# A two-layer hybrid flow-matching step: side tasks in smaller steps, a later deadline for modulations, and array tilings in the planner's estimate

## The chip, the cores and the metric

One core of one Trainium2 chip. The time is that of one execution in device microseconds (us); the median of several runs stands for a kernel. Engines are named as in the profile: PE (TensorE) multiplies, PEld is its weight load, DVE (VectorE), ACT (ScalarE) and POOL (GpSimd) do elementwise work, SP (SyncE) issues most of the DMAs.

## What is computed

Two layers run over 128 context tokens and 256 latent tokens, width 1024. A layer has a token mixer and a squared-ReLU MLP, each with an RMSNorm before and after it and with shift, scale and gain vectors ("modulations") that come from a condition vector:

```python
m = jax.nn.silu(cond) @ ada_w + ada_b        # six parts of 1024
h = rmsnorm(x, norm_mix_pre) * (1.0 + sc1) + sh1
y = mixer(h)                                 # z = h @ w_in, 12 branch inputs of 512, 4 gates of 1024
x = x + g1 * rmsnorm(y, norm_mix_post)
h = rmsnorm(x, norm_ffn_pre) * (1.0 + sc2) + sh2
x = x + g2 * rmsnorm(square(relu(h @ mlp_w1)) @ mlp_w2, norm_ffn_post)
```

The mixer has four branches: A, a neighbourhood attention; B, a differential attention; C, a retention in both directions, whose decay matrices are exponentials of distances; D, a short convolution over time followed by a gated linear recurrence (RG-LRU) in both directions. Each branch's result is multiplied by its own matrix `w_branch`, weighted with a sigmoid gate, and the sum goes through `w_out`.

## The kernel before, in words

All 384 tokens stay on the chip, mostly as channels by tokens. Float32 matrices are split into two parts of a faster type, a high part (wh) and the rest (wl), and each product is made of three matmuls (high by high, low by high, high by low). A weight load of 1 MB ("raw", two buffers) is split piece by piece: one copy for wh on ACT or DVE, one subtraction for wl on DVE or POOL (`split`, line 504).

The program is one list of pieces of weights, `run_stream` (line 626): for each piece the splits ahead of it are issued (`prepare`, `ahead`), its `pre` function, if it has one, is called, and then its matmuls are issued. A projection piece has 8 x 3 matmuls into one of two "mm" PSUM banks and then an eviction; a branch piece has two times 4 x 3 matmuls of 384 columns, each followed by an eviction (`acc` for branch B, `th` for the others). `triple` (line 865) yields after every 6 matmuls.

The mixer's order of pieces is: values of B, queries and keys of B, the convolution's input (`lx_evac`, line 1141), the LRU's gate (`lg_evac`), the retention's gate and values, gate and branch pieces of B ("yB"), queries and keys of C, gate and branch pieces of D ("yD"), values, queries and keys of A, gate and branch pieces of C ("yC") and of A ("yA"), and the output projection `add_out` (line 1573), whose last four pieces run with the norms that follow in `out_tail` (line 1592).

Everything else runs as side tasks: Python generators put into a list by `later` (line 587) with a tag and a capacity. After each yield of the matmuls `poll` (line 606) goes over the active tasks and advances each by one step, when what it needs is ready by the planner's own clock and when DVE and ACT are at most 2.25 us behind PE there; the tasks tagged "ada" come last and have a limit of their own. So a step's instructions stand in each engine's queue where the poll put them, and an eviction that follows in the program waits behind them. `drain_side(tag)` (line 619) advances tasks until none with the tag is left; `need_y` (line 1523) does so before the first branch piece of each branch. LRU tiles have capacity 7 and retention pairs 6 of the 8 that may be active together.

The planner's clock (`Clock`, and `Engine.cost` from line 167) gives each instruction a price. A matmul of plain float32 costs the larger of its columns / 585 and 0.22 us, and where it uses a part of the array that its caller names, this times its share of 128 output rows.

Side tasks that matter here:

- `lx_evac`: copies the bank to `xp` and runs the convolution, a TENSOR_SCALAR and three SCALAR_TENSOR_TENSOR on DVE, in the eviction itself.
- `lru_tile` (line 1188): per direction two times two matmuls on halves of the array, activations on ACT, products on DVE; then, in one step, for each direction a multiply and two scans on DVE, and two adds and two products.
- `ret_pair` (line 1290): the first step builds two decay matrices (four DVE operations, two exponentials on ACT) and the scaled queries.
- `ada` (line 779): the modulation vectors. For each of 8 x 2 blocks of a 1024-column part a load of 256 KB and two DVE accumulations, then `ada_end` with matmuls, transposes and small DMAs. The plan (line 1792) starts the parts 2, 3 and 4 of a layer within its mixer.
- `need_y` of the last branch also drains "ada", loads the three tiles of x (0.5 MB each) and the four gain tiles (0.25 MB each) through SP, and computes the scale columns.

Of the kernel before, what the change touches and what calls it, by code (L numbers as in the profile page):

```python
# [10 lines left out]
F32R = mybir.dt.float32r  # L11
# [122 lines left out]
def _size(a):  # L134
    n = 1
    for s in a.shape[1:]:
        n *= s
    return n


class Engine:


    def __init__(self, clock, raw, key):
        self.clock, self.raw, self.key = clock, raw, key

    def __getattr__(self, name):
# [19 lines left out]
    def cost(self, name, aps, k):  # L167
# [10 lines left out]
        if self.key == "PE":  # L178
            n = _size(aps[0])
            if name == "transpose":  # L180
                return 0.107
            if aps[1].dtype == F32R:
                return max(n / 2195, 0.107)
            return max(n / 585, 0.22) * (aps[0].shape[0] / 128 if "tile_position" in k else 1)
        if name == "reciprocal":
# [13 lines left out]
def hybrid_flow_kernel(ctx: ExitStack, tc: tile.TileContext, I, O):  # L199
# [734 lines left out]
    def add_layer(l):  # L934
# [206 lines left out]
        def lx_evac(j, p):  # L1141
            xp = atile()
            pool.memset(xp[:, 0:1], 0.0)
            pool.memset(xp[:, 129:131], 0.0)
            pool.memset(xp[:, 387:389], 0.0)
            dve.tensor_copy(xp[:, 1:129], p[:, 0:128])
            dve.tensor_copy(xp[:, 131:387], p[:, 128:384])
            xd = ctile("setB_x")
            cw = lambda i: P("pp")[:, R_CW + 4 * i + j:R_CW + 4 * i + j + 1]
            dve.tensor_scalar(xd[:, 0:NL], xp[:, 0:NL], cw(0), P("pp")[:, R_CB + j:R_CB + j + 1], op0=ALU.mult, op1=ALU.add)  # L1150
            for i in range(1, 4):
                dve.scalar_tensor_tensor(xd[:, 0:NL], xp[:, i:NL + i], cw(i), xd[:, 0:NL], op0=ALU.mult, op1=ALU.add)
            S["xd"][j] = xd

# [32 lines left out]

        def lru_tile(j):
            xd = S["xd"][j][:, 0:NL]
            while "kl" not in LP[l]:  # L1190
                yield
            yield (xd, *S["bia"])
# [33 lines left out]
            for d in range(2):  # L1226
# [4 lines left out]
                for s, init in ((slice(0, 128), 0.0), (slice(130, 386), st)):  # L1231
# [3 lines left out]
                    dve.tensor_tensor_scan(oo, aa, uu, init, ALU.mult, ALU.add)  # L1235
                hs.append(h)
            pool.tensor_copy(hst[:, j:j + 1], hs[0][:, 127:128])
            pool.tensor_copy(hst[:, 4 + j:5 + j], hs[1][:, 0:1])
            gg = S["gg"][j]
            for s, o in ((slice(0, 128), slice(0, 128)), (slice(130, 386), slice(128, 384))):  # L1240
                dve.tensor_add(hs[0][:, s], hs[0][:, s], hs[1][:, s])
                dve.scalar_tensor_tensor(gg[:, o], hs[0][:, s], 0.5, gg[:, o], op0=ALU.mult, op1=ALU.mult)
            S["yD"][j] = gg[:, 0:NTOK]
            if j == 3:
# [45 lines left out]
        def ret_pair(j):  # L1290
# [3 lines left out]
            for hh in range(2):  # L1294
# [5 lines left out]
                act(a, a, AF.Exp)  # L1300
                Dm.append(a)
            qx = []
            io = cst[:, C_IO:C_IO + 256]
# [202 lines left out]
        def add_gate_branch(bi, ykey, first, last):  # L1506
# [16 lines left out]
            def need_y():  # L1523
                drain_side(ykey)
                if last:
                    drain_side("ada")
                    S["X"] = [load_x_tile(l, t) for t in range(3)]
                    S["G"] = gain_tiles(l, 1)
                    S["A2"], S["B2"] = scale_cols(MOD[l, 4], pps[l], R_FFN), MOD[l, 3]

# [33 lines left out]
        def out_mm(k, t, hi, lo, banks=(0, 1)):  # L1564
            mh, ml = S["M"]
            tk = slice(t * 128, (t + 1) * 128)
            for n in banks:
# [3 lines left out]
                mm(p, mh[:, k, tk], wl, start=False, stop=k == KT - 1)  # L1571

        def add_out():
            def piece(k):
# [8 lines left out]
            for k in range(0, KT, 2):  # L1583
                src = I["w_out"][l][k * 128:(k + 2) * 128].rearrange("(k p) c -> p k c", p=128)
                add_load(src, lambda raw: raw.rearrange("p (k c) -> p k c", k=2),
                         [((lambda v, s=s: v[:, s]), (lambda t: t), piece(k + s), None)
                          for s in range(2)])
# [330 lines left out]
```

## Time and profile before

| | us |
|---|---|
| median of 3 runs | 1726.16 |
| lowest and highest run | 1722.91, 1727.71 |
| profiled execution, its own time | 1721.72 |
| its span in the profile | 1719.9 |
| PE busy in the span | 1661.3 |
| DVE busy | 1170.9 |
| ACT busy | 697.2 |

The profile is one execution. A line of it gives the time from the span's start, the duration, the engine, the operation, the tiles written and read, the shapes and a count; in square brackets stands how long the engine was idle before, and what ended that. The granted clock (PEclk) is TensorE's, as a share of full speed. All instructions come from one helper line (L151), so tiles tell them apart: `mm` and `y` are PSUM banks, `acc` and `th` evicted sums, `setB_x` the convolution's result, `tmp` working tiles, `half` and `big` the buffers of modulations, and x.

### The profile page before, as it was taken

The page shows a single profiled execution, that of the slowest core. Times are in us where ns is not written, and L with a number is a line of the kernel's source. Part 1 is how long each engine was busy: PE and PEld are TensorE (multiplying, and loading weights), DVE is VectorE, ACT ScalarE, POOL GpSimd, SP SyncE. Part 2 cuts the span into 40 slices and gives each one's busy share as a digit, 9 for nine tenths or more (in the row PEclk, how much of TensorE's full clock was granted, in tenths as well). Part 3 has the DMA queues.
Part 4 walks back from the last instruction along what each step waited for, and adds up shares of the span by engine and source line. Part 5 has one row for each costly group of instructions (what it writes and reads, how often), then busy time and mean ns, then how long its engine had stood idle before and what let it go on. Part 6 is the DMA issues. An engine that isn't in the chain of part 4 may idle for free.

```text
span 1719.9 us, 24255 instructions
## 1 busy us (share of the span) xinstructions
PE 1661.3 (97%) x9370; PEld 1492.2 (87%) x9370; DVE 1170.9 (68%) x2030; ACT 697.2 (41%) x1352; POOL 227.7 (13%) x298
## 2 busy tenths in 40 slices
PE   6999989999999999999999999999999999999998
PEld 4989879889789899898899887898888998898997
DVE  4586578998565746877677866787786666475444
ACT  4335555233332543333362446532343337333333
POOL 3211000322220100000021200013412101000000
PEclk8999999999999999999999999999999999999999
DMA  9432234458425425665453322453673442454332
GB/s 348 137 105 80 98 100 164 163 169 206 100 99 184 147 93 171 213 208 183 162 165 105 104 99 74 147 179 133 174 210 84 138 169 99 134 202 154 123 123 86
DMA packets 181124, 250.84 MB, mean 146 GB/s; under 512 B 21777, under 2 KB 126018, under 8 KB 181010
## 3 DMA queue, kind: packets, MB, share of 16 engines
q1 hardware_dynamic: 167234, 240.66, 41.1%
q0 software_dynamic: 3936, 5.94, 2.8%
q10 hardware_dynamic: 9840, 2.71, 0.7%
q8 instruction: 73, 1.20, 0.3%
q14 instruction: 41, 0.34, 0.1%
HBM read 243.47 MB, written 5.81 MB: 145 GB/s over the span
## 4 chain that ended last, share of the span: by engine, by line
PE 81%; DVE 8%; DMA 4%; ACT 3%; issue 3%; POOL 1%; SPq 0%; DVEq 0%; ACTq 0%; POOLq 0%
PE mm L151 48%; PE y L151 33%; DVE wl L151 2%; DMA half<-in_ada_w 2%; DVE tmp L151 2%; DVE big L151 1%; ACT tmp L151 1%; DMA half<-in_ada_b 1%; DMA wh<-in_ada_w 1%; ACT wh L151 1%; DVE half L151 1%; DVE setB_x L151 0%; ACT half L151 0%; DVE acc L151 0%; DVE small L151 0%
## 5 line engine op out<-in xcount | busy, mean ns | idle before, releaser
L151 PE MATMUL mm<-hh,wh 128*128 128x384 f32 x1536 | 537.2, 350 | 23.0 <-DVE acc L151 18.0
L151 PE MATMUL mm<-hh,wl 128*128 128x384 f32 x1536 | 520.7, 339 | 1.3 <-DVE wl L151 1.3
L151 PE MATMUL mm<-hl,wh 128*128 128x384 f32 x1536 | 520.4, 339 | 0.0
L151 DVE TENSOR_TENSOR wl<-raw,wh 128x1024 fp32r<-128x1024 f32 x313 | 394.4, 1262 | 163.2 <-ACT wh L151 155.5
L151 ACT ACTIVATE wh<-raw 128x1024 fp32r<-128x1024 f32 x249 | 262.2, 1055 | 224.9 <-PE y L151 139.7
L151 PEld LDWEIGHTS mm<-hh,wh 128*128 128x128 f32 x1536 | 290.7, 189 | 50.2 <-issue 21.1
L151 PEld LDWEIGHTS mm<-hl,wh 128*128 128x128 f32 x1536 | 290.6, 189 | 1.6
L151 PEld LDWEIGHTS mm<-hh,wl 128*128 128x128 f32 x1536 | 290.1, 189 | 1.6 <-DVE wl L151 1.6
L151 DVE SCALAR_TENSOR_TENSOR big<-half,condT,big 128x512 f32<-128x512 f32 x224 | 160.8, 755 | 15.0 <-DMA half<-in_ada_w 14.9
L151 PE MATMUL y<-wh,yh 128*128 128x512 f32 x312 | 123.4, 396 | 0.0
L151 PE MATMUL y<-wh,yl 128*128 128x512 f32 x312 | 123.4, 396 | 0.0
L151 PE MATMUL y<-wl,yh 128*128 128x512 f32 x312 | 123.3, 395 | 0.0
L151 PE MATMUL mm<-yh,wh 128*128 128x384 f32 x256 | 89.5, 350 | 3.2 <-DVE th L151 3.0
L151 POOL TENSOR_TENSOR small<-small,mhalf 128x1 f32<-128x1 f32 (+2 forms) x40 | 35.2, 883 | 413.2 <-DVE small L151 413.2
L151 DVE CAST wh<-raw 128x1024 fp32r<-128x1024 f32 x67 | 46.4, 692 | 61.0 <-PE mm L151 57.3
L151 PE MATMUL mm<-yh,wl 128*128 128x384 f32 x256 | 86.3, 337 | 0.0
L151 PE MATMUL mm<-yl,wh 128*128 128x384 f32 x256 | 86.2, 337 | 0.0
L151 ACT ACTIVATE tmp<-mm 128x384 f32<-128x384 f32 x64 | 31.4, 491 | 135.1 <-PE mm L151 135.1
L151 PE MATMUL y<-wh,hh 128*128 128x512 f32 (+1 forms) x192 | 76.0, 396 | 0.2 <-DVE hh L151 0.2
L151 PE MATMUL y<-wh,hl 128*128 128x512 f32 (+1 forms) x192 | 73.7, 384 | 0.3 <-DVE hl L151 0.3
L151 PE MATMUL y<-wl,hh 128*128 128x512 f32 (+1 forms) x192 | 73.6, 383 | 0.0
L151 PEld LDWEIGHTS y<-wl,yh 128*128 128x128 f32 x312 | 58.6, 188 | 14.1
(327 smaller groups left out, 2496.8 us busy)
## 6 DMA issues: line engine op xcount, KB each, us to landing
raw<-in_w_in SPq DMA_DIRECT2D x80, 1024.0 KB
raw<-in_mlp_w SPq DMA_DIRECT2D x64, 1024.0 KB
half<-in_ada_w SPq DMA_DIRECT2D x160, 256.0 KB
raw<-in_w_branch SPq DMA_DIRECT2D x16, 1024.0 KB
raw<-in_w_out SPq DMA_DIRECT2D x8, 1024.0 KB
v<-gscr SPq DMA_DIRECT2D x16, 256.0 KB
bia<-in_na_rpb POOLq DMA_DIRECT2D x32, 96.0 KB, 7.2
raw<-in_ada_w SPq DMA_DIRECT2D x4, 512.0 KB
```

What stands on the lines that cost most here:

```text
L151: r = f(*a, **k)
```

## The change

Four parts. LRU: the tile yields after each direction's scans and after each half of the final sum; it waits until its convolution is done. Convolution: it becomes a task of its own tag "yD" in two halves. Retention: a yield after each decay matrix. Deadline: what `need_y` of the last branch did besides draining its branch moves to `need_x`, the `pre` of the first piece of the output projection. And the planner's price of a PE instruction now knows which part of the array it uses: 0.1 us where that differs from the one before, 0.014 us beside an earlier one on another part, columns / 612 otherwise.

```diff
@@ class Engine
+        self.cut, self.places = (128, 128), []
@@ def cost
+            cut = tuple(next(x for x in (32, 64, 128) if a.shape[0] <= x) for a in (aps[1], aps[0]))
             if name == "transpose":
-                return 0.107
-            if aps[1].dtype == F32R:
-                return max(n / 2195, 0.107)
-            return max(n / 585, 0.22) * (aps[0].shape[0] / 128 if "tile_position" in k else 1)
+                cut = (128, 128)
+            place = (aps[1].start_partition(), aps[0].start_partition())
+            switch = 0.0 if cut == self.cut else 0.1
+            t = 0.107 if name == "transpose" else max(n / 2195, 0.107) if aps[1].dtype == F32R else max(n / 612, 0.22)
+            if switch or cut == (128, 128) or place in self.places:
+                self.places = []
+            beside = bool(self.places)
+            self.cut = cut
+            self.places.append(place)
+            return switch + (0.014 if beside else t)
@@ def lx_evac
             dve.tensor_copy(xp[:, 131:387], p[:, 128:384])
+            later(conv(j, xp), "yD")
+
+        def conv(j, xp):
+            yield (xp,)
             xd = ctile("setB_x")
...
             for i in range(1, 4):
                 dve.scalar_tensor_tensor(xd[:, 0:NL], xp[:, i:NL + i], cw(i), xd[:, 0:NL], op0=ALU.mult, op1=ALU.add)
+                if i == 1:
+                    yield
             S["xd"][j] = xd
@@ def lru_tile
+            while "kl" not in LP[l] or S["xd"][j] is None:
+                yield
             xd = S["xd"][j][:, 0:NL]
-            while "kl" not in LP[l]:
-                yield
...
                     dve.tensor_tensor_scan(oo, aa, uu, init, ALU.mult, ALU.add)
                 hs.append(h)
+                yield
...
                 dve.scalar_tensor_tensor(gg[:, o], hs[0][:, s], 0.5, gg[:, o], op0=ALU.mult, op1=ALU.mult)
+                yield
@@ def ret_pair
                 act(a, a, AF.Exp)
                 Dm.append(a)
+                yield
@@ def need_y
                 drain_side(ykey)
-                if last:
-                    drain_side("ada")
-                    S["X"] = [load_x_tile(l, t) for t in range(3)]
-                    S["G"] = gain_tiles(l, 1)
-                    S["A2"], S["B2"] = scale_cols(MOD[l, 4], pps[l], R_FFN), MOD[l, 3]
@@ before add_out
+        def need_x():
+            drain_side("ada")
+            S["X"] = [load_x_tile(l, t) for t in range(3)]
+            S["G"] = gain_tiles(l, 1)
+            S["A2"], S["B2"] = scale_cols(MOD[l, 4], pps[l], R_FFN), MOD[l, 3]
@@ def add_out
-                         [((lambda v, s=s: v[:, s]), (lambda t: t), piece(k + s), None)
+                         [((lambda v, s=s: v[:, s]), (lambda t: t), piece(k + s), None if k + s else need_x)
```

## Rows read from the trace of the kernel before

**Rows 1.** The page: busy us, share and instructions; the chain by engine.
```profile
PE 1661.3 (97%) x9370; PEld 1492.2 (87%) x9370; DVE 1170.9 (68%) x2030; ACT 697.2 (41%) x1352; POOL 227.7 (13%) x298
...
PE 81%; DVE 8%; DMA 4%; ACT 3%; issue 3%; POOL 1%; SPq 0%; DVEq 0%; ACTq 0%; POOLq 0%
```
**Rows 2.** Stretches: length, busy PE PEld DVE ACT POOL, PEclk, DMA share, GB/s.
```profile
200.00:265.00 65.00, 58.45 (x311) 47.55 (x311) 45.54 (x81) 37.85 (x62) 4.77 (x8) 0.95 0.33 110
...
640.00:875.00 235.00, 233.91 (x1174) 207.13 (x1173) 169.46 (x239) 89.65 (x137) 10.25 (x15) 1.00 0.56 189
```
**Rows 3.** Waits of PE, whole span: total us, times, longest.
```profile
PE mm L151 <- DVE acc L151: 18.0, 7, 3.9
```
**Rows 4.** PE's timeline: start, us, instruction, idle before and its end.
```profile
106.58 0.41 PE L151 MATMUL mm<-hh,wh 128*128 128x384 f32 x1 [1.49 <-DVE acc L151]
...
220.66 0.69 PE L151 MATMUL mm<-hh,wh 128*128 128x384 f32 x1 [3.28 <-DVE acc L151]
...
258.44 0.44 PE L151 MATMUL mm<-hh,wh 128*128 128x384 f32 x1 [3.27 <-DVE acc L151]
...
332.97 0.44 PE L151 MATMUL mm<-yh,wh 128*128 128x384 f32 x1 [1.06 <-DVE th L151]
...
1065.65 0.46 PE L151 MATMUL mm<-hh,wh 128*128 128x384 f32 x1 [3.92 <-DVE acc L151]
...
1102.48 0.44 PE L151 MATMUL mm<-hh,wh 128*128 128x384 f32 x1 [3.26 <-DVE acc L151]
...
1180.83 0.41 PE L151 MATMUL mm<-hh,wh 128*128 128x384 f32 x1 [2.06 <-DVE th L151]
```
**Rows 5.** DVE's timeline, 214 to 221.
```profile
214.48 1.23 DVE L151 TENSOR_TENSOR wl<-raw,wh 128x1024 fp32r<-128x1024 f32 x1 [0.68 <-ACT wh L151]
215.62 0.56 DVE L151 TENSOR_TENSOR tmp<-tmp 128x386 f32<-128x386 f32 x1
...
217.20 0.54 DVE L151 TENSOR_TENSOR tmp<-tmp 128x386 f32<-128x386 f32 x1
...
220.06 1.01 DVE L151 SCALAR_TENSOR_TENSOR acc<-th,mm 128x384 f32<-128x384 f32 x2
```
**Rows 6.** The chain that ended last, in order of time: start, us, what.
```profile
507.13 54.95 PE mm L151 x312
```
**Rows 7.** Stretches behind four waits, columns as in rows 2.
```profile
220.60:227.00 6.40, 6.34 (x20) 3.90 (x21) 2.65 (x5) 1.79 (x4) 0.00 (x0) 0.56 0.01 3
1065.60:1070.00 4.40, 4.34 (x15) 2.40 (x15) 1.74 (x4) 0.58 (x1) 0.00 (x0) 0.61 0.00 0
1102.40:1108.00 5.60, 5.52 (x23) 5.33 (x24) 3.12 (x6) 1.61 (x4) 0.90 (x1) 0.70 0.55 193
1180.80:1187.00 6.20, 6.17 (x28) 4.77 (x29) 3.56 (x9) 1.73 (x3) 4.35 (x4) 0.72 0.42 161
```
**Rows 8.** Tile acc, the convolution's products: count, ns min/median/max, first and last start.
```profile
L151 DVE SCALAR_TENSOR_TENSOR setB_x<-acc,pp,setB_x x24: 621/622/2650, 100.7 to 966.1; 128x386 f32<-128x386 f32 x24
```
**Rows 9.** POOL's timeline near 102.
```profile
101.81 2.54 POOL L151 TENSOR_TENSOR wl<-raw,wh 128x1024 fp32r<-128x1024 f32 x1 [5.52 <-ACT wh L151]
```
**Rows 10.** DVE's timeline at three moments of layer 0.
```profile
281.95 0.42 DVE L151 SCALAR_TENSOR_TENSOR setB_g<-tmp,setB_g 128x256 f32<-128x256 f32 x1
...
328.96 0.55 DVE L151 SCALAR_TENSOR_TENSOR th<-th,mm 128x384 f32<-128x384 f32 x1
...
440.04 1.42 DVE L151 SCALAR_TENSOR_TENSOR big<-half,condT,big 128x512 f32<-128x512 f32 x2 [6.35 <-DMA half<-in_ada_w]
```
**Rows 11.** SP's timeline, the first load of x in layer 0.
```profile
526.56 0.57 SPq L151 DMA_DIRECT2D big<-in_x_prompt  x1
```
**Rows 12.** ACT's timeline, the splits of the fourth w_out load.
```profile
573.50 2.05 ACT L151 ACTIVATE wh<-raw 128x1024 fp32r<-128x1024 f32 x2 [4.13 <-DMA raw<-in_w_out]
```
**Rows 13.** A stretch of the output projection, columns as in rows 2.
```profile
570.00:575.00 5.00, 5.00 (x24) 4.01 (x23) 1.27 (x3) 1.50 (x2) 0.00 (x0) 1.00 0.99 368
```
**Rows 14.** PE's timeline, one direction of an LRU tile.
```profile
202.57 1.51 PE L151 MATMUL y<-setB_x,bia 64*64 64x386 f32 x8
```

## Prediction

> **What bounds the kernel now.** I read the page first: busy times and the chain that ended last. TensorE is busy for 97% of the span and holds 81% of the chain [rows 1], so only time in which PE stands still, or runs slowly, can be won; DVE at 68% and ACT at 41% count only where PE waits for them. Second, the stretches: in the MLP PE is busy 233.91 of 235 us, while in the stretch that runs layer 0's LRU tiles beside the first gate and branch pieces it is busy 58.45 of 65 us at a granted clock of 0.95 [rows 2]. So the loss is local, in the mixer's side tasks. Third, PE's waits: the largest is 18.0 us in 7 waits for DVE's write of acc [rows 3], in most of them the instruction that empties one of the two "mm" banks. Fourth, PE's timeline with the waits one by one: four of the seven last 3.28, 3.27, 3.92 and 3.26 us, 13.7 together [rows 4], each in a branch piece of yB and each behind the same thing.
>
> That thing is on DVE's timeline [rows 5]. At 215.62 the last step of an LRU tile begins and runs without a break to the two acc evictions at 220.06: two multiplies, four scans, two adds and two products, 4.4 us in one step of the planner. PE takes 0.176 us for a matmul of this width (54.95 us for 312, in rows 6) and fills a bank in a branch piece with 12 of them, so 2.1 us; with two banks, an eviction that comes 4.4 us late must stop it. There are eight such bursts (four tiles, two layers); the other four stopped nothing for 3 us, since a projection piece gives its bank 24 matmuls.
>
> Fifth, the granted clock behind these waits: 0.56, 0.61 and 0.70 after three of the four [rows 7]. Part of each stretch is given the lower of the two levels, 1.2 GHz, after PE has stood idle for over 3 us. Lost: 6.4 x 0.44 + 4.4 x 0.39 + 5.6 x 0.30 = 6.2 us.
>
> **LRU in smaller steps.** The burst gets a yield after each direction's multiply and scans and after each half of the final sum. By rows 5 the first step is 1.58 us (215.62 to 217.20) and the second, the same work for the other direction, alike; the two sums share the remaining 1.3. An eviction of acc can now stand between them, since a poll comes every 6 matmuls and advances a task by one step, and a bank's eviction is issued behind every second poll. Replaying 215.62: step one ends at 217.20, the first eviction at 217.7, and PE, which stopped at 217.38 (220.66 less 3.28), goes on at about 217.8; the second bank is emptied behind step two at about 220, when PE has just filled the other. I keep 1.0 us of each wait: 13.7 - 4.0 = 9.7. Bounds: 0 (all steps still queue in front of one eviction) and 13.7. Of the dips' 6.2 I take 5, because a wait of 1.49 us at 106.58 [rows 4] is nearer to what I keep than the 3.28 that came before a dip; bounds 0 and 6.2.
>
> **Retention in smaller steps.** The first step of a pair builds two decay matrices in one go; now each has its own step. Two of PE's waits for DVE's th, 1.06 and 2.06 us, stand behind it [rows 4]. Half of the work in front goes: 1.6 of 3.1, and of the dip after the second (6.2 x 0.28 = 1.7, in rows 7) 1.2. Together 2.8; bounds 0 and 4.8.
>
> **The convolution as a task.** Its four DVE operations leave the eviction and follow at the next polls in two halves. What is left of the acc waits, 18.0 - 13.7 = 4.3 us in three, lies here. An operation of the convolution takes 622 ns in the median and once 2650 [rows 8]; the long one stood beside a weight split on GpSimd of 2.54 us [rows 9], and the eviction for which PE waited 1.49 us [rows 4] came behind it. I take that one, 1.5; bounds 0 (the next poll puts the halves in front of the same eviction) and 4.3. The Trainium skill, SBUF — State Buffer, under "Who interferes with whom", says that the pair of ports shared by VectorE and GpSimd is locked for a whole instruction, and against a VectorE operation with two SBUF inputs too. By that, whichever operation stands beside the split is held up, halves or not, so this term would be 0 and the sum 14.5 in place of 16.0; the long operation agrees with the lock, and no row shows the order that the change gives.
>
> **The deadline.** The drain of "ada", the three loads of x, the four gain loads and the scale columns go from the last branch's first piece to the first piece of the output projection, 192 matmuls or 34 us later. The drain is worth nothing: the last accumulation for layer 0's modulations in the mixer ends at 441.5 [rows 10], and PE runs on from 507.13 through the old place without a stop [rows 6]. What moves is 3 x 0.5 + 4 x 0.25 = 2.5 MB on SP's queue, from 526.56 [rows 11] to about 562, behind the third w_out load and ahead of the fourth. That fourth load is already awaited by ACT for 4.13 us [rows 12], and behind it come the first MLP weights, which ACT and DVE split around the post norm. At 368 GB/s [rows 13] 2.5 MB is 6.8 us. PE did not stop for those 4.13 us, and a few more of the kind stay under the products of the output projection; I take 0.75 us a layer, 1.5 lost; bounds 0 and 2 x 6.8 = 13.6. Where the loads lay, nothing stalled, so nothing is won there.
>
> **The ordering estimate.** No instruction changes for it; PE's simulated clock does, and so which poll advances a task. The eight matmul passes of an LRU direction take 1.51 us in the trace [rows 14]; the old formula gives 4 x 0.33 = 1.32, the new 0.1 + 2 x 0.645 = 1.39. Tenths of a microsecond in a few dozen places move tasks by a poll, and other waits by a little either way: 0, with ends of 4 us won or lost, about the length of one of the longest waits of rows 4.
>
> **Added steps.** An LRU tile needs four more polls, a retention pair two. Tiles and pairs can't be active together (capacities 7 and 6 of 8), so the first pairs of layer 0 come later. That tile work ends at 282.4, and yD is drained before the branch whose first eviction is at 328.96 [rows 10], 46 us on; 16 steps at one or two polls of 1.05 us are 17 to 34, so the cover holds; without it the rest of a tile would run with PE idle. For small steps in front of other evictions I take off 1.5 us, the price of one wait like that of 106.58; bounds 0 and 4.
>
> **Sum.** 9.7 + 5.0 + 2.8 + 1.5 - 1.5 - 1.5 = 16.0 us less. The profiled execution took 1721.7 us, so 1705.7; the median of the three runs is 4.4 above it, so I forecast 1710 us. About 0.3%, 5 us, is what a measurement can tell from no change.
>
> **Rivals.**
> - Forecast, the bursts are divided: 11 to 22 us won, 1704 to 1715. Chance 0.70.
> - The loads of x collide. If the 2.5 MB land whole before the fourth w_out load, its splits and the post norm behind them are 6.8 us later in each layer: 16.0 + 1.5 - 13.6 = 3.9 won, 1722. For it: the queue's order, and DMA nearly full there [rows 13]. Against it: the norm's first token is followed by other tokens' products, on which PE can go on. Chance 0.10.
> - The change doesn't do what it says: the planner's DVE clock sees no backlog and the polls lay the steps back to back in front of the same evictions. LRU and convolution give nothing, retention 2.8, the loads and steps take 3.0: 1726. For it: the planner didn't foresee the four waits either. Against it: by program order, not by its clock, an eviction comes behind every second poll of a branch piece. Chance 0.11.
> - Slower: the wait is multiplied. In branch pieces a weight split (1.23) and a step (1.58) in front of an eviction exceed the 2.1 - 0.5 us that a bank leaves, by 1.2 us; the pieces which the other four bursts used to miss are now met as well. It decides once the 32 steps stop PE for more than (13.7 + 6.2) / 32 = 0.62 us each; at 0.9 it is 28.8 - 19.9 = 8.9 slower, 1735. For it: every step now has an eviction close behind. Against it: half of the steps are below 0.8 us. Chance 0.09.
>
> The range reaches from 1701, the forecast's end with most of the order's 4 us, to 1725, which takes in the first rival and ends at the second; the forecast's own is 1704 to 1715. Faster: 0.70 and half of the first rival (it lies at the edge), 0.75; same: its other half and most of the second, 0.15; slower: 0.10.
>
> **What would show it.** Right: no PE wait for acc above 1.5 us in the yB branch pieces, acc evictions on DVE between the scans of one tile, a granted clock of 1.00 after them; the loads of x behind the third w_out load, and PE without a stop until the post norm. Wrong: four or more waits over 3 us left there; ACT waiting over 6 us for w_out or MLP weights after 570; an LRU step forced in front of the yD branch.

## The result and the profile after

| | before | after |
|---|---|---|
| median, us (runs) | 1724.54 (4) | 1696.50 (4) |
| lowest and highest run | 1721.38, 1727.71 | 1695.86, 1697.74 |
| profiled execution, its own time | 1721.72 | 1696.75 |
| its span | 1719.9 | 1695.0 |
| PE busy in the span | 1661.3 | 1653.9 |

The ratio of the times is 0.9838 (interval 0.9817 to 0.9859): 28 us less by the medians, 25.0 by the two profiled executions. The forecast was 1710 with a range from 1701 to 1725, so the direction was right and the gain nearly twice as large as the one forecast.

The page of the kernel after, its lines of busy times and of the chain's shares; instructions now come from L152:

```profile
PE 1653.9 (98%) x9370; PEld 1488.0 (88%) x9370; DVE 1157.9 (68%) x2033; ACT 704.0 (42%) x1358; POOL 210.1 (12%) x289
...
PE 89%; DVE 5%; ACT 2%; DMA 2%; issue 1%; POOL 0%; SPq 0%; ACTq 0%; DVEq 0%; POOLq 0%
```

PE runs the same 9370 matmuls as in [rows 1]. Its share of the chain rises from 81 to 89%, and what DVE, DMA and ACT held shrinks. The span lost 24.9 us: 17.5 of them are time without a matmul (span less busy: 58.6 before, 41.1 after), 7.4 are less busy time for the same matmuls.

Stretches of the kernel after, columns as in [rows 2]; the first and the last answer to those rows, the two between them are the two moments at which the clock is still low between the start and the last 2 us:

```profile
198.00:263.00 65.00, 62.96 (x348) 54.30 (x347) 50.35 (x91) 42.74 (x69) 5.27 (x9) 1.00 0.40 130
325.00:331.00 6.00, 6.00 (x33) 3.93 (x29) 4.26 (x11) 0.00 (x0) 2.54 (x2) 0.74 0.20 77
1217.00:1224.00 7.00, 6.16 (x26) 6.16 (x27) 6.79 (x9) 1.54 (x3) 1.58 (x3) 0.76 0.45 153
640.00:875.00 235.00, 235.00 (x1222) 208.86 (x1221) 174.65 (x256) 94.73 (x155) 15.38 (x29) 1.00 0.56 192
```

The stretch with layer 0's LRU tiles has PE busy for 62.96 of 65 us in place of 58.45, at a granted clock of 1.00 in place of 0.95. The MLP, where little was to be won, changes by 1.1 us of PE's busy time.

Waits of PE over the whole span of the kernel after (total us, times, longest):

```profile
PE mm L152 <- DVE th L152: 7.1, 8, 1.8
...
PE y L152 <- DVE half L152: 2.9, 5, 1.3
PE mm L152 <- DVE acc L152: 2.8, 4, 1.5
PE mm L152 <- DVE wl L152: 2.6, 1, 2.6
```

The waits for acc fell from 18.0 us [rows 3] to 2.8. The second line is one that the prediction had no row for, PE's waits for "half", the buffer in which a modulation ends. Here they are 2.9 us; in the trace of before they were the next largest behind those for acc:

```profile
PE y L151 <- DVE half L151: 6.9, 7, 3.1
```

DVE's timeline of the kernel after, around a tile that answers to the burst of [rows 5]:

```profile
238.36 0.56 DVE L152 TENSOR_TENSOR tmp<-tmp 128x386 f32<-128x386 f32 x1 [0.52 <-ACT tmp L152]
238.96 0.42 DVE L152 TENSOR_TENSOR_SCAN tmp<-tmp 128x128 f32<-128x128 f32 x1
239.30 0.72 DVE L152 TENSOR_TENSOR_SCAN tmp<-tmp,pp 128x256 f32<-128x256 f32 x1
239.94 0.53 DVE L152 SCALAR_TENSOR_TENSOR acc<-th,mm 128x384 f32<-128x384 f32 x1
240.39 0.55 DVE L152 TENSOR_TENSOR tmp<-tmp 128x386 f32<-128x386 f32 x1
...
242.26 0.29 DVE L152 SCALAR_TENSOR_TENSOR setB_g<-tmp,setB_g 128x128 f32<-128x128 f32 x1
242.47 0.55 DVE L152 SCALAR_TENSOR_TENSOR acc<-th,mm 128x384 f32<-128x384 f32 x1
...
244.06 0.42 DVE L152 TENSOR_TENSOR tmp<-tmp 128x256 f32<-128x256 f32 x1
```

This is the forecast's picture: an eviction of acc at 239.94 between the two directions' scans, another at 242.47 between the two halves of the sum. PE's timeline of the kernel after has these waits of more than 1.2 us from 50 us on:

```profile
207.99 0.44 PE L152 MATMUL mm<-yh,wh 128*128 128x384 f32 x1 [1.50 <-DVE acc L152]
...
317.02 0.44 PE L152 MATMUL mm<-yh,wh 128*128 128x384 f32 x1 [1.56 <-DVE th L152]
323.27 0.41 PE L152 MATMUL mm<-hh,wh 128*128 128x384 f32 x1 [1.75 <-DVE th L152]
423.24 0.55 PE L152 MATMUL y<-ident,setB_g 128*128 128x128 f32 x3 [1.28 <-ACT tmp L152]
...
1217.84 0.44 PE L152 MATMUL mm<-hh,wl 128*128 128x384 f32 x1 [2.57 <-DVE wl L152]
...
1228.07 0.66 PE L152 MATMUL y<-ident,half 128*128 128x128 f32 x4 [1.29 <-DVE half L152]
```

None of the four waits above 3 us of [rows 4] is left, and 1.50 us is the longest for acc.

Where the time was won: the wide matmuls of the streamed pieces (384 and 512 columns on the full array) have the same order in both kernels, so the k-th of them can be subtracted, one trace from the other. The LRU stretches give 8.0 us in layer 0 (200 to 300 in the trace of before) and 9.6 in layer 1 (1060 to 1108), 17.6 together; the prediction's LRU terms with their dips made 14.7. The norms behind the output projection lose 1.9 in each layer. Around the end of a modulation (440 to 450 in layer 0) another 5.8 are won, and layer 1's branches of C and A lose and win by turns as tasks move. This says where the time was won, not by which part of the change: the price alone wins in layer 0's LRU stretch too, as an experiment below shows.

### The profile page after: what moved, and what is told of

Read it like the earlier page. It is cut to its first block, busy times and chain, and to the rows that moved or that the text cites. A ratio compares the mean times of both kernels' runs of the same rounds, so it can differ in the third digit from the quotient of the medians.

```text
span 1695.0 us, 24214 instructions
## 1 busy us (share of the span) xinstructions
PE 1653.9 (98%) x9370; PEld 1488.0 (88%) x9370; DVE 1157.9 (68%) x2033; ACT 704.0 (42%) x1358; POOL 210.1 (12%) x289
## 4 chain that ended last, share of the span: by engine, by line
PE 89%; DVE 5%; ACT 2%; DMA 2%; issue 1%; POOL 0%; SPq 0%; ACTq 0%; DVEq 0%; POOLq 0%
PE mm L152 54%; PE y L152 35%; DVE big L152 1%; DVE tmp L152 1%; DVE wl L152 1%; DMA half<-in_ada_w 1%; ACT half L152 1%; DMA wh<-in_ada_w 1%; ACT tmp L152 0%; ACT wh L152 0%; DVE half L152 0%; DMA ident<-in_const 0%; DVE hl L152 0%; DVE small L152 0%; DVE th L152 0%
## 5 line engine op out<-in xcount | busy, mean ns | idle before, releaser
L152 PE MATMUL mm<-hh,wh 128*128 128x384 f32 x1536 | 534.6, 348 | 4.0 <-DVE th L152 3.2
L152 PE MATMUL mm<-hh,wl 128*128 128x384 f32 x1536 | 518.4, 338 | 2.6 <-DVE wl L152 2.6
L152 DVE TENSOR_TENSOR wl<-raw,wh 128x1024 fp32r<-128x1024 f32 x316 | 396.0, 1255 | 180.1 <-ACT wh L152 170.0
L152 PE MATMUL mm<-hl,wh 128*128 128x384 f32 x1536 | 518.2, 337 | 0.0
L152 ACT ACTIVATE wh<-raw 128x1024 fp32r<-128x1024 f32 x260 | 273.7, 1055 | 217.6 <-PE y L152 139.2
L152 PEld LDWEIGHTS mm<-hh,wh 128*128 128x128 f32 x1536 | 289.6, 189 | 28.9 <-issue 18.4
L152 PEld LDWEIGHTS mm<-hh,wl 128*128 128x128 f32 x1536 | 289.0, 188 | 2.9 <-DVE wl L152 2.9
L152 PEld LDWEIGHTS mm<-hl,wh 128*128 128x128 f32 x1536 | 289.5, 189 | 1.6
L152 DVE SCALAR_TENSOR_TENSOR big<-half,condT,big 128x512 f32<-128x512 f32 x224 | 162.4, 764 | 16.0 <-DMA half<-in_ada_w 16.0
L152 PE MATMUL y<-wh,yh 128*128 128x512 f32 x312 | 123.8, 397 | 0.0
L152 PE MATMUL y<-wl,yh 128*128 128x512 f32 x312 | 123.7, 396 | 0.0
L152 PE MATMUL y<-wh,yl 128*128 128x512 f32 x312 | 123.5, 396 | 0.0
L152 PE MATMUL mm<-yh,wh 128*128 128x384 f32 x256 | 90.2, 352 | 5.9 <-DVE th L152 3.9
L152 POOL TENSOR_TENSOR small<-small,mhalf 128x1 f32<-128x1 f32 (+2 forms) x40 | 36.2, 906 | 431.3 <-DVE small L152 431.2
L152 PE MATMUL mm<-yl,wh 128*128 128x384 f32 x256 | 86.7, 339 | 0.0
L152 PE MATMUL mm<-yh,wl 128*128 128x384 f32 x256 | 86.6, 338 | 0.0
L152 ACT ACTIVATE tmp<-mm 128x384 f32<-128x384 f32 x64 | 31.5, 492 | 132.2 <-PE mm L152 132.2
L152 DVE CAST wh<-raw 128x1024 fp32r<-128x1024 f32 x56 | 40.9, 729 | 55.5 <-PE mm L152 53.9
L152 PE MATMUL y<-wh,hh 128*128 128x512 f32 (+1 forms) x192 | 75.1, 391 | 0.2 <-DVE hh L152 0.2
L152 PE MATMUL y<-wh,hl 128*128 128x512 f32 (+1 forms) x192 | 73.4, 382 | 0.3 <-DVE hl L152 0.3
L152 PE MATMUL y<-wl,hh 128*128 128x512 f32 (+1 forms) x192 | 73.3, 382 | 0.0
L152 PEld LDWEIGHTS y<-wl,yh 128*128 128x128 f32 x312 | 58.7, 188 | 14.3
```

The source lines that it names most:

```text
L152: r = f(*a, **k)
```

## The experiments

Sixteen kernels. They differ in the order of the work, and in which engine the planner gives a split or a copy. "Undone" is the changed kernel less one part, "alone" is the kernel before with one part. Ratios are to the kernel before, run on the same chip, each with its interval; that of the whole change is 0.9838.

**Undone: the LRU's steps.**

```diff
                 hs.append(h)
-                yield
...
                 dve.scalar_tensor_tensor(gg[:, o], hs[0][:, s], 0.5, gg[:, o], op0=ALU.mult, op1=ALU.mult)
-                yield
```

> The changed kernel with the LRU tile's last step whole again. Theory 1 (the divided bursts are worth the whole of their waits and of the dips behind them, 13.7 + 6.2 us, not the 14.7 that I forecast): 19 us back, 1716 us, with four PE waits for acc over 3 us. Theory 2 (the surplus comes from the order that the new estimate gives): only the forecast's 10 to 13 us back, 1707 to 1710.

Measured: 1708.18 us, ratio 0.9918 (0.9898 to 0.9937): 12 us above the changed kernel by the medians, 14 by the ratios. PE's waits for acc in this kernel:

```profile
PE mm L152 <- DVE acc L152: 11.0, 4, 3.2
```

and, on PE's timeline, the three of them over 2.4 us:

```profile
247.22 0.44 PE L152 MATMUL mm<-yh,wh 128*128 128x384 f32 x1 [2.41 <-DVE acc L152]
...
1055.74 0.69 PE L152 MATMUL mm<-hh,wh 128*128 128x384 f32 x1 [3.12 <-DVE acc L152]
...
1093.56 0.69 PE L152 MATMUL mm<-hh,wh 128*128 128x384 f32 x1 [3.18 <-DVE acc L152]
```

The waits for acc come back with the long step. That the undivided step makes them is shown.

**Undone: the new price of a PE instruction.**

```diff
...
-            return switch + (0.014 if beside else t)
...
+            return max(n / 585, 0.22) * (aps[0].shape[0] / 128 if "tile_position" in k else 1)
```

> The changed kernel with the old price of a PE instruction. Theory 1: the estimate is worth the 2.3 us that the two traces differ by before the first side task, plus or minus 3 of reordering: 1696 to 1702. Theory 2: it carries the surplus over my forecast, 8 to 12 us: 1705 to 1709.

Measured: 1709.83 us, 0.9925 (0.9907 to 0.9943), 13 to 15 us more. It is worth as much as the LRU's steps, and the prediction had it at nothing. Waits of PE in this kernel:

```profile
PE y L151 <- DVE half L151: 9.8, 7, 5.2
...
PE y L151 <- DVE big L151: 3.4, 1, 3.4
PE mm L151 <- DVE acc L151: 3.4, 5, 1.5
```

The waits for acc stay short; those for half and big are 13.2 us against 3.5 in the changed kernel (2.9, and 0.6 for big). Both are the end of a modulation: a product with "ones" adds the partitions of big, DVE adds the bias into half, and PE transposes half. PE's timeline at two of these ends, in layers 0 and 1:

```profile
432.98 2.58 PE L151 MATMUL y<-big,ones 128*32 128x512 f32 x4 [3.39 <-DVE big L151]
...
439.10 1.12 PE L151 MATMUL y<-ident,half 128*128 128x128 f32 x4 [1.32 <-DVE half L151]
...
1281.28 1.11 PE L151 MATMUL y<-ident,half 128*128 128x128 f32 x4 [5.24 <-DVE half L151]
```

DVE's timeline at the first of them, the accumulation that big waits for:

```profile
432.18 1.42 DVE L151 SCALAR_TENSOR_TENSOR big<-half,condT,big 128x512 f32<-128x512 f32 x2 [6.70 <-DMA half<-in_ada_w]
```

and the stretches around the two, columns as in [rows 2]:

```profile
430.00:440.00 10.00, 5.70 (x15) 3.05 (x15) 6.29 (x14) 1.42 (x4) 3.14 (x4) 0.61 0.40 130
1278.00:1288.00 10.00, 6.72 (x33) 6.60 (x34) 5.24 (x15) 3.99 (x10) 3.07 (x4) 0.66 0.73 135
```

DVE stands 6.70 us for the last 256 KB of ada_w, and PE, whose queue already holds the product with ones, stands behind it for 3.39 us; then it runs on with a granted clock of 0.61. The planner had put both instructions there: it advances "ada" when its PE clock has passed the landing of the load by its own reckoning. The second of the two is not a late load: DVE was busy with other tasks up to half at 1280.55, though the product that it reads had ended at 1274.78. The changed kernel's product with ones at 450.36 and its transposes at 452.52 have no idle time in front of them. By the k-th matmul, the new price wins 7.7 us around the first end (420 to 470 in this experiment's trace) and 14.9 around the second (1240 to 1320), and loses 10 elsewhere.

**Undone: the later deadline.** `need_x` removed, its lines back in `need_y`.

```diff
+                if last:
+                    drain_side("ada")
+                    S["X"] = [load_x_tile(l, t) for t in range(3)]
...
-        def need_x():
-            drain_side("ada")
...
```

> The changed kernel with the old, early place for the drain, the loads of x and the gains. The traces differ by 1.9 us a layer against the change in the norms behind the output projection. If that is the moved loads, undoing it wins 3 to 4 us: 1693. If it is the new estimate or the DVE order, it stays: 1696 to 1698. If the deadline itself was worth something, it is slower than 1700.

Measured: 1692.09 us, 0.9821 (0.9802 to 0.9840), 4.4 us faster than the changed kernel by the medians (all four runs lie below all four of it) and 2.9 by the ratios, whose intervals overlap. By these runs and by the traces this part costs time. SP's timeline of the changed kernel, as [rows 11]:

```profile
547.59 0.46 SPq L152 DMA_DIRECT2D big<-in_x_prompt  x1
548.10 1.12 SPq L152 DMA_DIRECT2D big<-in_x_sample  x2
549.26 1.95 SPq L152 DMA_DIRECT2D v<-gscr  x4
553.58 0.38 SPq L152 DMA_DIRECT2D raw<-in_w_out  x1
```

and ACT's behind it, as [rows 12]:

```profile
561.54 2.01 ACT L152 ACTIVATE wh<-raw 128x1024 fp32r<-128x1024 f32 x2 [7.23 <-DMA raw<-in_w_out]
```

ACT waits 7.23 us for the fourth load of w_out where it waited 4.13 before, and 4.14 in this experiment. PE loses 1.9 us of that in each layer, at the norms behind the products; undone, 2.0 and 1.6 come back there.

**Undone: the convolution's task.** Its four operations back in `lx_evac`.

```diff
-            later(conv(j, xp), "yD")
-
-        def conv(j, xp):
-            yield (xp,)
...
-                if i == 1:
-                    yield
...
```

> The changed kernel with the convolution back in the eviction. Theory 1: the first layer's stretch from the convolution to the retention's values, 3.9 us faster in the trace, is the convolution's, the second layer's 0: 3 to 5 us back, 1700 to 1702. Rival (the lock on the shared port decides, halves or not): within 1.5 us, 1695 to 1698.

Measured: 1702.72 us, 0.9881 (0.9863 to 0.9900): 6 us more by the medians, 7 by the ratios. DVE's timeline of this experiment in layer 0:

```profile
98.17 4.04 DVE L152 SCALAR_TENSOR_TENSOR setB_x<-acc,pp,setB_x 128x386 f32<-128x386 f32 x3
102.13 1.21 DVE L152 TENSOR_TENSOR wl<-raw,wh 128x1024 fp32r<-128x1024 f32 x1
```

and GpSimd's beside it:

```profile
99.24 2.55 POOL L152 TENSOR_TENSOR wl<-raw,wh 128x1024 fp32r<-128x1024 f32 x1 [4.74 <-ACT wh L152]
```

Three products that take 2.00 us elsewhere (at 952.32) take 4.04 beside a split on GpSimd, as in [rows 8, 9], and 4.23 at 945.79 beside one that starts at 947.22. PE stops behind them for 2.28 us at 104.88 and for 2.05 at 951.84. The kernel before had both bursts too, one in each layer: 4.04 us at 100.73, with the wait of 1.49 behind it [rows 4], and, beside a split on GpSimd that starts at 958.26,

```profile
958.62 4.03 DVE L151 SCALAR_TENSOR_TENSOR setB_x<-acc,pp,setB_x 128x386 f32<-128x386 f32 x3
```

with a wait of PE of 1.38 us behind it, at 964.24. In the changed kernel the tile view gives the same products so:

```profile
L152 DVE SCALAR_TENSOR_TENSOR setB_x<-acc,pp,setB_x x24: 614/622/623, 101.9 to 962.6; 128x386 f32<-128x386 f32 x24
```

The longest is 623 ns: no split on GpSimd stands beside any of them. With the convolution's tasks in other places the planner put all splits of these stretches (96 to 125, 935 to 970) on other engines.

**Undone: retention's step.**

```diff
                 Dm.append(a)
-                yield
```

> The changed kernel with the retention's two decay matrices in one step again. If the split wins its waits (2.8 us forecast), 2 to 4 us back: 1698 to 1701. Rival (the two halves are polled one after the other in front of the same evictions; the two traces differ by +4 us in layer 0's retention and -5 in layer 1's): within 2 us, 1695 to 1698.

Measured: 1699.83 us, 0.9861 (0.9846 to 0.9876), 3 to 4 us more: all four runs lie above all four of the changed kernel, though the intervals overlap.

**Alone: the LRU's steps; the price; both together.** The kernel before with the first of these edits, with the second, and with both.

```diff
                 hs.append(h)
+                yield
...
                 dve.scalar_tensor_tensor(gg[:, o], hs[0][:, s], 0.5, gg[:, o], op0=ALU.mult, op1=ALU.mult)
+                yield
```
```diff
-            return max(n / 585, 0.22) * (aps[0].shape[0] / 128 if "tile_position" in k else 1)
...
+            return switch + (0.014 if beside else t)
```

> The kernel before with only the LRU tile's yields added. Theory 1 (each part wins its own waits): the four waits of 13.7 us and their dips go, 15 to 19 us won, 1703 to 1707. Theory 2 (the parts need each other: later order decides a good part): 8 to 12 us won, as undoing it cost 11.7 us, 1710 to 1714; the four waits are gone from the trace all the same, and others appear behind.

> The kernel before with only the new price of a PE instruction. Theory 1: the waits behind the LRU bursts stay, so at most the 9 to 13 us that undoing it cost in the changed kernel, by the waits for modulations near 440 and 1285: 1709 to 1713. Theory 2 (a price moves tasks by a poll and the gain is the luck of one order): 1717 to 1727, and the waits near 440 and 1285 stay or move.

> The kernel before with the LRU tile's yields and the new price, nothing else. Each alone won 17 and 10 us. If they save different waits: 27 us, 1695. If they overlap (in the trace of the estimate alone, layer 0's two LRU waits are gone too, 12 of its 10 to 17 us): 17 to 21 us, 1701 to 1705, and the convolution's stretches keep their waits of 1 to 2.6 us for acc.

Measured: 1705.12 us, 0.9903 (0.9882 to 0.9925) for the steps, 17.1 less than the kernel before beside it; 1711.82, 0.9945 (0.9924 to 0.9967), 10.4 less, for the price; 1697.42, 0.9858 (0.9835 to 0.9882), 26.8 less, for both. On top of the steps the price wins 7.7. The two gains add up (27.5), and these two parts are nearly the whole change: it is another 0.9 us lower by the medians, less than these runs tell apart.

That they add up does not mean that they win different waits. PE's timeline with the price alone still has layer 1's pair of [rows 4]:

```profile
1054.79 0.44 PE L152 MATMUL mm<-hh,wh 128*128 128x384 f32 x1 [3.26 <-DVE acc L152]
...
1091.68 0.44 PE L152 MATMUL mm<-hh,wh 128*128 128x384 f32 x1 [3.35 <-DVE acc L152]
```

Layer 0's pair is gone, though its bursts are undivided: they fall between the evictions (DVE's scans of the first three run from 205.24 to 207.86, from 221.99 to 224.60 and from 237.04 to 239.66, the evictions of acc from 211.09 to 219.31 and from 242.89 to 251.11). The stretch that answers to the first of [rows 2], in the kernel with the price alone, has no idle time of PE at all:

```profile
198.00:263.00 65.00, 65.00 (x365) 57.25 (x362) 50.22 (x89) 45.41 (x72) 5.75 (x10) 1.00 0.31 101
```

By the k-th matmul (198 to 300 in the trace of before) the price alone wins 12.7 us there, the steps alone 5.7, both 13.0. So in layer 0 the two overlap by 5.4 us, and that the sum comes out all the same is luck: from 300 to 360 the price alone loses 4.7, the steps alone 0.4, and both together only 0.7. Nor does the price alone shorten PE's waits for half, 6.9 us before (it wins 7.6 us from 420 to 470, but 2.81 and 3.15 us stand in layer 1):

```profile
PE mm L152 <- DVE acc L152: 13.0, 6, 3.4
PE y L152 <- DVE half L152: 7.9, 6, 3.1
```

**The price taken apart.** In the changed kernel: no 0.1 us for a change of the array's part; 0.3 in its place; no cheap instruction beside another (the old share of rows instead); 585 columns for 612; and the old price times 0.75.

```diff
-            switch = 0.0 if cut == self.cut else 0.1
+            switch = 0.0
```
```diff
-            switch = 0.0 if cut == self.cut else 0.1
+            switch = 0.0 if cut == self.cut else 0.3
```
```diff
-            return switch + (0.014 if beside else t)
+            return switch + t * (aps[0].shape[0] / 128 if "tile_position" in k else 1)
```
```diff
-            t = 0.107 if name == "transpose" else max(n / 2195, 0.107) if aps[1].dtype == F32R else max(n / 612, 0.22)
+            t = 0.107 if name == "transpose" else max(n / 2195, 0.107) if aps[1].dtype == F32R else max(n / 585, 0.22)
```
```diff
...
-            return switch + (0.014 if beside else t)
...
+            return 0.75 * max(n / 585, 0.22) * (aps[0].shape[0] / 128 if "tile_position" in k else 1)
```

> The changed kernel with the 0.1 us for a change of the array's parts set to 0 in the price. If the truth of the estimate matters, about 150 changes of 0.1 us a layer make the planner's clock run early and cost a few us: 1699 to 1705. If the estimate's gain is the luck of one order, the time falls anywhere between the changed kernel and the one with the old price, 1694 to 1710, with waits for ada_w moved.

> The changed kernel with 0.3 us for a change of parts, three times what the trace shows (270 against 175 ns between matmuls). If the truth of the price matters, the planner's clock runs late and the time goes the old price's way: 1700 to 1708. If not, 1692 to 1699.

> The changed kernel with columns / 585 in place of columns / 612, everything else of the new price kept: 0.02 to 0.06 us on some hundred matmuls. If the truth of the price matters, nothing: 1695 to 1698. If the order's luck does, more than 3 us either way, with the difference in the waits for ada_w.

> The changed kernel whose price has the 0.1 us for a change of parts and columns / 612, but charges a matmul beside another on its own part as before. If the estimate's gain comes from knowing that matmuls run beside each other (neighbourhood scores, retention scores, LRU, modulations), most of the 13 us that the old price cost comes back: 1704 to 1711. If any new price would do, 1694 to 1699.

> The old price times 0.75 for every plain float32 matmul: too low for those that stand alone, nearly right for those beside each other. If an error either way costs, 1704 to 1712. If only a price that is too high for matmuls beside each other costs (loads are thought to have landed that haven't), it is near the changed kernel: 1694 to 1701.

To see which price is wrong where, take the products beside which the modulations end, those of branch A's attention. PE's timeline with the old price:

```profile
1264.89 0.71 PE L151 MATMUL y<-setB_g,setB_x 64*128 64x256 f32 x4
```

These are two matmuls (one of plain float32 has two records: 128 records for the 64 that the LRU issues), beside each other on halves of the rows, in 0.71 us. The old price for them is 2 x 256 / 585 = 0.875, the new one 0.1 + 256 / 612 + 0.014 = 0.53; the others follow in the same way.

| price of a PE instruction | the pair, us | median, us | ratio (interval) | PE's waits for half, us |
|---|---|---|---|---|
| change of part 0 | 0.43 | 1698.15 | 0.9859 (0.9839 to 0.9879) | 1.7 |
| new | 0.53 | 1696.50 | 0.9838 (0.9817 to 0.9859) | 2.9 |
| 585 columns | 0.55 | 1694.03 | 0.9842 (0.9818 to 0.9866) | 1.6 |
| old times 0.75 | 0.66 | 1699.45 | 0.9869 (0.9849 to 0.9890) | 4.7 |
| change of part 0.3 | 0.73, and 0.3 to change back | 1709.04 | 0.9923 (0.9901 to 0.9945) | 7.9 |
| old | 0.875 | 1709.83 | 0.9925 (0.9907 to 0.9943) | 9.8 |
| none beside | 0.94 | 1701.30 | 0.9869 (0.9855 to 0.9884) | 12.4 |

Above the trace's 0.71 us for the pair (0.73 is hardly above it, but for the 0.3 to change back), PE waits 7.9 to 12.4 us for half and the kernel takes 5 to 13 us more than the changed one; below it the waits are 1.6 to 4.7 us and the time lies within 3. Within the upper group neither the error nor the waits order the times: the longest waits, 12.4 us, go with the shortest time. By the k-th matmul that kernel loses 22 us at the two ends of modulations, as the one with the old price does, and wins 18 elsewhere. These products are not the only ones whose price moves, so the pair as the cause is argued; that the price decides is shown.

Not all came as expected. The few us that a price without the change of part was to cost did not come (1698.15), 585 columns (1694.03) ended 1 us below the range for no effect and short of the 3 us that the other reading asked for, and none beside ended between its two (1701.30). So a price nearer to the trace is not by itself a faster kernel; here only the prices above the trace cost more than 3 us.

**Luck of one order?** If the price only shuffled tasks, another shuffle would do the same. Both kernels were run with another small price of the planner, 0.25 for 0.2 us from DVE to the next engine.

```diff
-    HOP = dict(PE=0.1, ACT=0.14, DVE=0.2, POOL=0.06, SP=0.0)
+    HOP = dict(PE=0.1, ACT=0.14, DVE=0.25, POOL=0.06, SP=0.0)
```

> The changed kernel with the planner's delay behind a DVE result at 0.25 in place of 0.20 us. Nothing in it bears on the array. If the new price's gain holds for any order, 1693 to 1701. If it was the luck of one order, anywhere from 1694 to 1712.

> The same other delay under the old price (e2 with 0.25 us). If the old price is what costs, 1706 to 1713. If e2's 1710 was an unlucky order, anywhere from 1694 to 1712.

Measured: 1696.40 us, 0.9848 (0.9827 to 0.9870), with the new price; 1711.10, 0.9937 (0.9917 to 0.9956), with the old. They stay 15 us apart. With the old price PE again waits 10.8 us for half and 5.0 for big; with the new one it waits 5.9 for half, the longest 3.8, and none for big over 0.6. By the k-th matmul the new price wins 4.2 and 10.9 us around the two ends, as with the other delay. With the price alone and on top of the LRU's steps that makes four pairs of kernels, 7.7 to 14.7 us apart, all in the same direction: one lucky order is not the reason. Which waits go is another matter; it differs from pair to pair.

**A version that beats both.** The deadline as before, one more load of ada_w in flight, and each accumulation of a modulation taken up 3 us after the landing that the planner reckons.

```diff
-    ADA_LOADS = 3
+    ADA_LOADS = 4
...
-                    yield (raw,)
+                    yield (clock.at((raw,)) + 3.0,)
...
```

> A version meant to beat both: x early as in e3, four loads of modulation weights in flight, and an accumulation is polled only 3 us after its load is due by the planner. If DVE's waits for ada_w (17 us in the changed kernel's trace, with PE behind the longest) are what is left, 4 to 8 us below e3's 1692: 1684 to 1688. If that idle time is covered or the fourth load crowds the weights, 1690 to 1694.

Measured: 1689.95 us, 0.9804 (0.9788 to 0.9819): 34 us below the kernel before and 6 to 7 below the changed one, all four runs below all four of it. It does not reach the 1684 to 1688 that were hoped for. The group of DVE's accumulations (busy, mean ns, then its idle time in front of them) in the changed kernel:

```profile
L152 DVE SCALAR_TENSOR_TENSOR big<-half,condT,big 128x512 f32<-128x512 f32 x224 | 162.4, 764 | 16.0 <-DMA half<-in_ada_w 16.0
```

and in this one:

```profile
L152 DVE SCALAR_TENSOR_TENSOR big<-half,condT,big 128x512 f32<-128x512 f32 x224 | 166.1, 780 | 7.3 <-DMA half<-in_ada_w 7.3
```

DVE stands 7.3 us for these loads in place of 16.0, and PE's waits for half fall from 2.9 to 1.9 us. Of the 6 to 7 us, 4.4 are the deadline's (the experiment above); the 2 that are left for the margin and the fourth load together are about as large as what such runs can tell, and which of the two makes them was not tested.

## Why the prediction was wrong in size

**The ordering estimate is the step that failed.** The prediction put it at "0, with ends of 4 us won or lost", because no instruction changes for it. It is worth 10.4 us alone, 7.7 on top of the LRU's steps, and 13 to 15 undone, two to nearly four times the end of its range. Two things were wrong. It took "about the length of one of the longest waits" as the most that moved tasks can win: with the price alone, two of the four longest waits, 3.28 and 3.27 us, go at once, and layer 0's LRU stretch wins 12.7 us. And it looked at PE's waits for acc and th alone. PE's waits for half were the next largest of before, 6.9 us; at the end of layer 0's modulation PE was busy for 6.03 us of a stretch of 10, in the trace of before:

```profile
440.00:450.00 10.00, 6.03 (x27) 3.75 (x28) 6.39 (x14) 1.42 (x4) 3.10 (x4) 0.91 0.34 110
```

The prediction read DVE's accumulation there [rows 10], its 6.35 us of waiting for ada_w in plain sight, and concluded for the deadline that nothing stalled, since PE runs on from 507. But PE's timeline, in the same stretch, has this:

```profile
446.93 0.66 PE L151 MATMUL y<-ident,half 128*128 128x128 f32 x4 [3.12 <-DVE half L151]
```

The same stretch in the changed kernel, two us later:

```profile
442.00:452.00 10.00, 10.00 (x72) 8.24 (x71) 5.89 (x11) 4.84 (x15) 1.12 (x2) 1.00 0.43 127
```

What is shown: the price is worth 7.7 to 14.7 us in four settings of the rest, at the ends of modulations in the two where it is undone, and in layer 0's LRU stretch as well where it stands alone. Why a price does so is not shown. It is argued from `poll` that a PE clock that runs ahead in the plan makes loads look landed, so that the instructions of a modulation's end are queued too early; the products that make it run ahead would be the pairs of branch A's attention, which fall from 0.875 to 0.53, from above the trace to below it, where the prediction reckoned only with an LRU direction (1.32 by the old price, 1.39 by the new). Against a simple account: DVE's idle time in front of the accumulations is 20.7 us with the old price and 16.0 with the new, but 21.1 with the change of part at 0, which is nearly as fast as the new. So it is not DVE's wait by itself that costs.

**LRU in smaller steps**: right in mechanism, too small in size. The terms were 9.7 and 5.0, less 1.5 for added steps, 13.2; alone the steps give 17.1, undone they cost 12 to 14. In the changed kernel the waits of [rows 4] went below the 1.0 us each that was kept (0.81 us at 1046.52, under 0.5 in the others of the yB pieces but the 1.50 at 207.99), though the price has a share in that; with the steps alone one of 1.97 us is left, at 221.14. Behind them the clock is at 1.00 in place of 0.56, 0.61 and 0.70 [rows 7]. A small slip in the reading: the four waits stand not in a branch piece but at the first matmul of the gate piece behind it (`mm<-hh`), which waits for the branch piece's evictions; the argument is the same.

**The convolution**: 1.5 forecast, 6 to 7 measured undone. The prediction read the largest of [rows 8], 2650 ns, as the only long product and tied it to layer 0's split. There are two, 2.64 us in layer 0 and 2.65 in layer 1, and the waits behind their bursts are 1.49 and 1.38 us; with the convolution undone in the new order they are 2.28 and 2.05. The rule of the Trainium skill, SBUF — State Buffer, "Who interferes with whom", agrees with the two long bursts (4.04 and 4.23 us beside splits of 2.55 and 2.40); what was drawn from it, that the term is 0, does not hold, since the moved tasks moved the splits as well.

**Retention**: 2.8 forecast, 3.3 by the medians. **The deadline**: the sign and the place were right, a cost of 1.5 forecast, 2.9 to 4.4 measured; its wrong-signal, ACT over 6 us for w_out, is there (7.23), and costs 1.9 us a layer where the rival had 6.8. **The offset** of 4.4 us between the profiled execution and the median of before was carried over to the kernel after, whose median is 0.25 us below its profiled execution; so 4.6 of the 13.5 us of error come from there, and 9.0 from the sum (16.0 for 25.0).

Undone one at a time, the five parts are worth 11.7, 13.3, 6.2, 3.3 and -4.4 us by the medians, 30 in all against 28.0 for the whole: they nearly add up. That the two large ones alone already give 26.8 leaves some 4 us open, about what one such comparison can tell. By the k-th matmul, the changed kernel wins 7.5 us at the convolution (97 to 198) over the kernel with these two, but loses 8.1 from 198 to 360 and 3.6 at the norms; why it loses in the first of these stretches was not tested.

No rival came: the loads collide at a third of their price, the bursts are divided, and no wait was multiplied (PE's waits for th are 7.1 us in all, 6.6 before).

## What to carry to other kernels

A planner's price list is part of the kernel: no instruction changes with it, and it was worth 8 to 15 us here, about as much as the best edit of the code. In this kernel the lists with a price above the trace's duration for a pair of products cost 5 to 13 us and those below it at most 3, so prices are compared with the trace shape by shape; that the lower one is the safer holds for the seven lists that were run, and the reason for it is argued. Before an edit is priced at nothing because no instruction changes, go down the list of waits to the second and third line and ask which of them it could move, and how many at once. Two gains that add up may still have been won at the same place: subtract the traces stretch by stretch before calling them independent. When a step of a side task is cut, look at what an eviction behind it waited for; when a load is moved, look at which load stands behind it in the queue.

## What was not expected of the hardware

The length of one idle time does not tell whether the clock falls. In the trace of before PE stood 3.28 us at 220.66 and ran on at 0.56, and 3.27 us at 258.44 [rows 4] and ran on at full clock:

```profile
258.40:264.00 5.60, 5.56 (x31) 4.36 (x32) 4.58 (x9) 3.32 (x7) 0.07 (x1) 1.00 0.83 286
```

In the kernel after, 1.50 us at 207.99 left the clock at 1.00, and 1.56 and 1.75 us within 7 us of each other (317.02, 323.27) were followed by 0.74 from 325 to 331. So the prediction's "after PE has stood idle for over 3 us" is no rule: the dip behind 1180.83 [rows 7] followed a wait of 2.06 us, and one of 1.51 at 1176.41.
